# Hybrid block on one core: paired subtractions, gate parts on ScalarE and a deeper ring of raw weights in a linear-attention kernel

## The chip, the core and the metric

The program runs on 1 core of one Trainium2 chip. It uses TensorE (PE, matrix products; its weight loads are listed apart as PEld), VectorE (DVE), ScalarE (ACT), GpSimd (POOL) and the DMA queue of SyncE (SP). Each engine works through its own list of instructions in order and waits where one of them needs a result of another engine. The metric is the device time of the whole program in microseconds (us), as the median of several runs.

## The reference

Two transformer blocks follow each other on 512 tokens of width 1024. The first has two feed-forward layers and, between them, a mixer over 512 latent tokens and 256 context tokens. Half of that mixer is an HGRN2 linear attention with 4 heads of 128 channels, run in both directions. The second block has a Mamba2 mixer, a sparse attention and a mixture of experts. What the change touches computes this, for each head and direction:

```
q     = silu(hg_q) * 128 ** -0.5
log_f = log(lb + (1 - lb) * sigmoid(f_pre))
k_in  = (1 - lb) * sigmoid(-f_pre)
# per chunk, in token order:
b      = cumsum(log_f)
decay  = exp(b[t] - b[s])            for s <= t
scores = einsum('td,tsd,sd->ts', q, decay, k_in)
o      = scores @ v + (q * exp(b)) @ state
state  = exp(b_last) * state + (k_in * exp(b_last - b)).T @ v
```

The parts of the second block that matter here are `ada = silu(c) @ w_ada + b_ada` (a row of 6144 numbers out of a weight of 1024 x 6144) and its norm and projections `(rmsnorm(h) * (1 + scale) + shift) @ w_in`.

## The kernel before

Activations lie transposed, channels on the partitions and tokens along the row. Every large product is done as three products of split operands (`mm3`, L212 to L214): a weight is loaded as `wraw` (L183), rounded to `whi` on ACT (L193), and its rest `wlo` is formed on DVE (L194). The order of the instructions on each engine comes from a list scheduler that runs over the whole program with estimated durations and priorities (`later`, `high_priority`), so that an edit in one place can move instructions of other places.

**The HGRN2 stage** (`mix1`, 860 to 1120 us) goes through the 4 heads. `hg_front` (L881 to L943) makes for one head the projections, the gates and their prefix sums, in two directions `d`; `hg_back` (L945 to L1108) makes the attention. While `hg_back` of one head runs, `hg_front` of the next is in the lists too.

In `hg_front` the projection of the forget gate lands in two PSUM tiles, one of 512 latent and one of 256 context tokens. With p for it, DVE writes min(p, 0) and min(-p, 0) into slots 0 and 1 of `W` (L911, L912), ACT takes the exponential of both in one instruction of 1536 columns (L914), POOL adds them into slot 2 (L915), DVE writes slot 1 times lb plus slot 0 into slot 0 (L916), and ACT takes the logarithm of slots 0 and 2 (L917). DVE then reads p again (L921), which frees the PSUM tile, and forms log_f (L922), its prefix sum (`tensor_tensor_scan`, L927 or L932) and the second array (L929 or L934). Both land in one tile `BA` of four rows.

In `hg_back` the 512 x 512 decay is not formed. Seven levels m = 64, 32, ..., 1 split the sequence in blocks of 2m tokens; in each, queries of one half meet keys of the other, both measured from the border between them. For m < 64, two DVE subtractions fill the two halves of a tile `z` of 512 columns (L979, L980; the second reference is subtracted the other way round), ACT takes the exponential of the whole tile (L982), DVE multiplies the query half by q (L983), and PE does small products of `z` with itself (L988, L993, L999). DVE masks the small ones (L1003) and sums them (L1082), POOL copies the sums into the score tile (L1084), and PE finishes the head (L1089 to L1091), after which a norm follows (`hsq`, L1094; `rstdl`, L314; `rstd`, L319; `ho`, L1099). Six levels in two directions and four heads give 48 pairs of subtractions.

ACT keeps a table for the functions in use. A logarithm after an exponential, or the other way round, stands behind an ACT_TABLE_LOAD where the compiled list has one.

**The stage behind it** (1120 to 1200 us) finishes the mixer's output and computes the remaining rows of `ada`: `matvec` (L259 to L288) loads pieces of 512 KB into a ring of `mraw` tiles in the pool `xq` (L241), and PE multiplies them (L267). The ring has 6 tiles there (`MR = 6`). Two further parts of the row, `ada_row`, 8 pieces in all, run after the second feed-forward layer (L1809, L1816), at the start of the sparse attention near 1550 us, where the copy of their sums, `mvs`, is on ACT (L250). The memory of `xq` is used again by the tiles of the sparse attention, among them the weights `cw` (L1511).

Of the kernel before, what the change touches and what calls it, by code (L numbers as in the profile page):

```python
# [15 lines left out]
AF = mybir.ActivationFunctionType  # L16
OP = mybir.AluOpType
# [13 lines left out]
L = 512  # L31
C = 256
T = L + C
# [455 lines left out]
XA, XU, HPL = 0, 1, ()  # L489


class Mix1:
# [391 lines left out]
    def hg_front(self, i, w, vec, h):  # L884

        nc, hs = self.nc, self.hs
        PE = lambda k: nc.gpsimd if k in HPL else nc.vector
        lb = vec["lb"]
        q = hs.tile([128, L], F32, name="q", bufs=2)
        g = hs.tile([128, L], F32, name="g", bufs=2)  # L890

        def act(dst):
            def ev(p, t0, n):
                nc.scalar.activation(dst, p, AF.Tanh, scale=0.5)
                nc.vector.scalar_tensor_tensor(dst, dst, 1.0, p, op0=OP.add, op1=OP.mult)
            return ev
        self.proj_T(self.wsplit(self.cols(w, h * 128, 128), [8, 128], 2 in WL), self.LAT, act(q))

        BA = hs.tile([128, 4, T], F32, name="BA", bufs=2)
        Tt = hs.tile([128, 2, 12], F32, name="Tt", bufs=2)  # L900
        ks = hs.tile([128, L], F32, name="ks", bufs=2)
        for d in range(2):
            wt = self.wsplit(self.cols(w, 1536 + d * 512 + h * 128, 128), [8, 128], 3 + d in WL)
            col = slice(d * 4 + h, d * 4 + h + 1)
            W = hs.tile([128, 1 + 3 * T], F32, name="W", bufs=1)
            Wv = W[:, 1:].rearrange("p (s t) -> p s t", s=3)
            ps = []

            def evf(p, t0, n):
                ps.append((p, t0, n))  # L910
                nc.vector.tensor_scalar(Wv[:, 0, t0:t0 + n], p, 0.0, None, op0=OP.min)  # L911
                nc.vector.tensor_scalar(Wv[:, 1, t0:t0 + n], p, -1.0, 0.0, op0=OP.mult, op1=OP.min)  # L912
            self.proj_T(wt, self.ALL, evf)
            nc.scalar.activation(Wv[:, 0:2], Wv[:, 0:2], AF.Exp)  # L914
            nc.gpsimd.tensor_tensor(Wv[:, 2], Wv[:, 0], Wv[:, 1], op=OP.add)  # L915
            nc.vector.scalar_tensor_tensor(Wv[:, 0], Wv[:, 1], lb[:, col], Wv[:, 0], op0=OP.mult, op1=OP.add)  # L916
            nc.scalar.activation(Wv[:, 0:3:2], Wv[:, 0:3:2], AF.Ln, bias=self.tiny)  # L917
            lf, nk = Wv[:, 0], Wv[:, 1]
            for p, t0, n in ps:
                s = slice(t0, t0 + n)  # L920
                nc.vector.scalar_tensor_tensor(nk[:, s], p, 0.0, Wv[:, 2, s], op0=OP.max, op1=OP.add)  # L921
            PE(("l", d)).tensor_tensor(lf, lf, Wv[:, 2], op=OP.subtract)  # L922
            B, A = BA[:, 1 + d], BA[:, 3 * d]
            B64 = B.rearrange("p (b t) -> p b t", t=64)
            lno = vec["lno"][:, col]
            if d == 0:
                nc.vector.tensor_tensor_scan(B, self.rst64, lf, 0.0, op0=OP.mult, op1=OP.add)  # L927
                nc.vector.tensor_copy(Tt[:, d], B64[:, :, 63])
                nc.vector.scalar_tensor_tensor(A, nk, lno, B, op0=OP.subtract, op1=OP.add)  # L929
            else:  # L930
                nc.gpsimd.memset(W[:, 0:1], 0.0)
                nc.vector.tensor_tensor_scan(B, W[:, 0:T], self.rst64, 0.0, op0=OP.add, op1=OP.mult)  # L932
                nc.vector.tensor_add(Tt[:, d], B64[:, :, 63], lf.rearrange("p (b t) -> p b t", t=64)[:, :, 63])
                nc.vector.scalar_tensor_tensor(A, B, lno, nk, op0=OP.add, op1=OP.subtract)  # L934

            k = ks if d == 0 else Wv[:, 1, :L]
            nc.scalar.activation(k, nk[:, :L], AF.Exp, scale=-1.0, bias=lno)
            if d == 1:
                PE("k").tensor_tensor(ks, ks, k, op=OP.add)
        self.proj_T(self.wsplit(self.cols(w, 1024 + h * 128, 128), [8, 128], 5 in WL), self.LAT, act(g))  # L940
        for _ in range(FB[1]):
            self.filler()
        return q, g, BA, Tt, ks  # L943

    def hg_back(self, vec, h, mrg, front):  # L945
        nc, hs = self.nc, self.hs
        PE = lambda k: nc.gpsimd if k in HPL else nc.vector
        q, g, BA, Ta, ks = front
# [7 lines left out]
        for d in range(2):  # L956
            B, A, Tt = BA[:, 1 + d, :L], BA[:, 3 * d, :L], Ta[:, d, :8]
            X, Y = BA[:, 2 * d, :L], BA[:, 2 * d + 1, :L]
            sq, sk = (1, 0) if d == 0 else (0, 1)
            pds = [self.pt("pb") for _ in range(2)]  # L960
            nl = 6 - d
            for li, m in enumerate(LV + ([0] if d == 0 else [])):
                if m:
                    zz = hs.tile([128, L], F32, name="z", bufs=ZB)
                    half = lambda t: t.rearrange("p (b u t) -> p b u t", u=2, t=m)
                    zv, v, x, y = half(zz), half(B), half(X)[:, :, 0, :], half(Y)[:, :, 1, :]
                    nb = L // (2 * m)
                    if m == 64:
                        tv = Tt.rearrange("p (b u) -> p b u", u=2)
                        nc.vector.tensor_tensor(zv[:, :, 0, :], tv[:, :, 0:1].to_broadcast([128, nb, m]), x, op=OP.subtract)  # L970
                        if XA:
                            nc.scalar.activation(zv[:, :, 1, :], y, AF.Exp)
                            nc.scalar.activation(zv[:, :, 0, :], zv[:, :, 0, :], AF.Exp)
                        else:
                            nc.gpsimd.tensor_copy(zv[:, :, 1, :], y)
                    else:
                        r = v[:, :, 0, m - 1:m] if d == 0 else v[:, :, 1, 0:1]
                        r = r.to_broadcast([128, nb, m])
                        PE(("x", d, m)).tensor_tensor(zv[:, :, 0, :], r, x, op=OP.subtract)  # L979
                        PE(("y", d, m)).tensor_tensor(zv[:, :, 1, :], y, r, op=OP.subtract)  # L980
                    if m != 64 or not XA:
                        nc.scalar.activation(zz, zz, AF.Exp)  # L982
                    PE(("q", d, m)).tensor_tensor(zv[:, :, sq, :], zv[:, :, sq, :], half(q)[:, :, sq, :], op=OP.mult)  # L983
                for c in range(4):
                    t0 = c * 128
# [9 lines left out]
                    else:  # L995
                        x = ((c % 2) * nl + li - 2) * 32
                        for b in range(4):
                            s = slice(t0 + b * 32, t0 + b * 32 + 32)
# [40 lines left out]
            else:  # L1039
                nc.vector.memset(off[:, 0], 0.0)  # L1040
                for b in (1, 2, 3):
# [3 lines left out]
                                    op=OP.subtract if d == 0 else OP.add)  # L1045
# [13 lines left out]
            p = self.pt("pb")  # L1059
# [7 lines left out]
            for a, b in zip(order[:-1], order[1:]):  # L1067
                n = cs.index(a)
                nc.vector.scalar_tensor_tensor(st[:, b, :], st[:, a, :], eT[:, a:a + 1], p[:, n * 128:(n + 1) * 128],
                                               op0=OP.mult, op1=OP.add)  # L1070
# [9 lines left out]
        for half in range(2):  # L1080
            r = hs.tile([128, 2, 32], F32, name="dr", bufs=2)
# [1259 lines left out]
MA = (0, 1)  # L2341
# [22 lines left out]
class Top:  # L2364
# [41 lines left out]
    def first(self, i, b1, lat, mrg, xd, x1d, cosd, sind, row):  # L2406
# [107 lines left out]
        with tc.tile_pool(name="xq", bufs=1, reuse_waits="tile") as xq:  # L2514
# [1 line left out]
            for o in range(KC):  # L2516
                nc.sync.dma_start(xT[:, o, :], xd[:, o, :])
            out_half(0, lambda o: xT[:, o, :], lambda o, x: None, OA)
            self.mvp, self.ptag, self.mva = xq, "pb", MA[0]
            for f in self.fill + [row.pop(0) for _ in range(FN)]:  # L2520
                f()
            a, b = scales(6, "n3", 1)
# [65 lines left out]
```

## Time and profile before

| | |
|---|---|
| median of 3 runs | 2819.61 us (2817.72 to 2821.18) |
| profiled execution, its own time | 2824.22 us |
| span of its profile | 2822.4 us |
| busy over the span: PE / DVE / ACT / POOL | 94% / 55% / 35% / 10% |
| granted TensorE clock, mean | 0.975 of full speed |
| DMA | 380.46 MB, mean 135 GB/s |

The page divides busy time by the whole span, and stages with different limits are mixed in it: DVE has 55% over all, and much more in some stretches. So the stretches are read one by one, by the busy time of each engine between two times, and then by what each engine waited for there. In the timelines a row shows the start, the duration, the engine, the line, the operation and the tiles; behind it in brackets stands the idle time before it and the instruction that ended it. An instruction's duration overlaps with the start of the next, so that the distance between two starts is what one costs its engine.

### The profile page before, as it was taken

To read this page: it belongs to the slowest core of one execution; us is meant where nothing else is said; L and a number is where in the kernel's file an instruction comes from. 1 tells how busy PE (TensorE), PEld (TensorE's weight loads), DVE (VectorE), ACT (ScalarE), POOL (GpSimd) and SP (SyncE) were. 2 spreads that over 40 slices of the span, in tenths; PEclk is the share of its full clock that TensorE was granted. 3 is DMA by queue.
4 is the path that set the end of the run, shared out by engine and by line. 5 is a ranking of instruction groups with operands and counts; after the bars stand their busy time and mean duration, and the time that the engine had idled before them with its cause. 6 is when DMAs were issued, how large, how long until landed. Compare 5 with 4: busy or idle time off the path is not lost. (4 is left out here: it accounts for less than half of the span.)

```text
span 2822.4 us, 40841 instructions
## 1 busy us (share of the span) xinstructions
PE 2666.9 (94%) x16161; PEld 2055.5 (73%) x16162; DVE 1549.1 (55%) x3025; ACT 995.6 (35%) x1796; POOL 279.3 (10%) x319
## 2 busy tenths in 40 slices
PE   7999999999998887999999899999999989979998
PEld 5788888888887765678888678777777767854443
DVE  6333333338367885554434757676667764454444
ACT  5211112225235663422222424465444443231112
POOL 2000000002001210100000101121122230010000
PEclk9999999999999988999999999999999999989999
DMA  7422122134333228732333523301234358269995
GB/s 263 150 90 68 58 63 67 46 98 119 98 104 100 65 81 268 254 97 90 98 96 87 153 83 98 92 13 36 76 104 123 97 185 256 82 228 368 368 359 213
DMA packets 341571, 380.46 MB, mean 135 GB/s; under 512 B 21881, under 2 KB 252669, under 8 KB 341122
## 3 DMA queue, kind: packets, MB, share of 16 engines
q1 hardware_dynamic: 339074, 373.63, 41.1%
q0 software_dynamic: 2304, 4.20, 0.5%
q8 instruction: 128, 2.10, 0.3%
q14 instruction: 65, 0.53, 0.1%
HBM read 352.34 MB, written 29.63 MB: 135 GB/s over the span
## 5 line engine op out<-in xcount | busy, mean ns | idle before, releaser
L193 ACT CAST whi<-wraw 128x1024 fp32r<-128x1024 f32 x277 | 285.8, 1042 | 742.4 <-PE pppa L213 332.5
L212 PE MATMUL pppa<-lath,whi 128*128 128x512 f32 (+4 forms) x1344 | 522.4, 390 | 18.2 <-ACT lath L1835 5.0
L213 PE MATMUL pppa<-latl,whi 128*128 128x512 f32 (+3 forms) x1344 | 520.0, 387 | 6.4 <-DVE latl L360 4.3
L214 PE MATMUL pppa<-lath,wlo 128*128 128x512 f32 (+3 forms) x1344 | 513.3, 384 | 0.0
L194 DVE TENSOR_TENSOR wlo<-wraw,whi 128x1024 fp32r<-128x1024 f32 (+1 forms) x273 | 332.9, 1225 | 244.4 <-ACT whi L193 239.8
L212 PEld LDWEIGHTS pppa<-lath,whi 128*128 128x128 f32 (+3 forms) x1344 | 256.1, 191 | 81.4 <-ACT whi L193 10.8
L213 PEld LDWEIGHTS pppa<-latl,whi 128*128 128x128 f32 (+2 forms) x1344 | 255.6, 190 | 63.4 <-DVE latl L360 7.6
L214 PEld LDWEIGHTS pppa<-lath,wlo 128*128 128x128 f32 (+2 forms) x1344 | 255.2, 190 | 50.9 <-issue 2.8
L213 PE MATMUL pppb<-hl,whi 128*128 128x512 f32 (+1 forms) x576 | 195.6, 341 | 0.0
L212 PE MATMUL pppb<-hh,whi 128*128 128x512 f32 (+1 forms) x576 | 193.2, 345 | 0.0
L214 PE MATMUL pppb<-hh,wlo 128*128 128x512 f32 (+1 forms) x576 | 190.9, 340 | 0.0
L418 DVE SCALAR_TENSOR_TENSOR xT<-pppb,sG,xT 128x512 f32<-128x512 f32 (+1 forms) x144 | 96.7, 689 | 137.4 <-PE pppb L214 137.3
L398 DVE TENSOR_TENSOR hf<-sg,pppa 128x256 f32<-128x256 f32 (+1 forms) x68 | 39.6, 583 | 228.6 <-PE pppa L214 227.3
L212 PE MATMUL pppf<-lath,whi 128*128 128x512 f32 x320 | 128.0, 400 | 6.9 <-ACT lath L1835 3.1
L212 PE MATMUL pppa<-ctxh,whi 128*128 128x256 f32 (+1 forms) x440 | 124.0, 282 | 7.0 <-DVE W L921 7.0
L212 PEld LDWEIGHTS pppb<-hh,whi 128*128 128x128 f32 x576 | 108.2, 189 | 28.1 <-issue 5.8
L2143 PE MATMUL pppa<-ew,xg 128*64 128x512 f32 x512 | 128.4, 607 | 0.0
L214 PE MATMUL pppf<-lath,wlo 128*128 128x512 f32 x320 | 126.7, 396 | 0.6 <-DVE wlo L194 0.6
L213 PE MATMUL pppf<-latl,whi 128*128 128x512 f32 x320 | 126.8, 396 | 0.1
L213 PE MATMUL pppa<-ctxl,whi 128*128 128x256 f32 (+1 forms) x440 | 123.6, 281 | 0.4 <-POOL ctxl L358 0.4
L214 PE MATMUL pppa<-ctxh,wlo 128*128 128x256 f32 (+1 forms) x440 | 123.5, 281 | 0.0
L213 PEld LDWEIGHTS pppb<-hl,whi 128*128 128x128 f32 x576 | 108.9, 189 | 15.6 <-issue 3.4
(694 smaller groups left out, 4985.4 us busy)
## 6 DMA issues: line engine op xcount, KB each, us to landing
wraw<-in_ffn_w_dram SPq DMA_DIRECT2D x132, 512.0 KB, 4.0
wraw<-in_w_in_dram SPq DMA_DIRECT2D x102, 512.0 KB, 4.0
ew<-in_w_exp_gate_dram SPq DMA_DIRECT2D x64, 512.0 KB, 8.6
ew<-in_w_exp_up_dram SPq DMA_DIRECT2D x64, 512.0 KB, 4.8
ew<-in_w_exp_down_dram SPq DMA_DIRECT2D x32, 1024.0 KB, 11.0
mraw<-in_w_mod_dram SPq DMA_DIRECT2D x40, 512.0 KB, 6.2
wraw<-in_w_mod_dram SPq DMA_DIRECT2D x32, 512.0 KB, 4.2
mraw<-in_w_ada_dram SPq DMA_DIRECT2D x32, 512.0 KB, 5.6
```

Source lines behind the costliest of these rows:

```text
L193: nc.scalar.copy(hi[:, :n], raw[:, :n])
L194: (nc.gpsimd if pool else nc.vector).tensor_sub(lo[:, :n], raw[:, :n], hi[:, :n].bitcast(F32))
L212: nc.tensor.matmul(out, wh, xh, start=start, stop=False)
L213: nc.tensor.matmul(out, wh, xl, start=False, stop=False)
L214: nc.tensor.matmul(out, wl, xh, start=False, stop=stop)
L398: nc.vector.tensor_mul(h[:, :n], sg[:, :n], pp[1])
L418: nc.vector.scalar_tensor_tensor(x[:, o, :], p[:, :n], gate[:, o:o + 1], x[:, o, :], op0=OP.mult, op1=OP.add)
L2143: nc.tensor.matmul(ph[x * 64:x * 64 + 64, :], xg[:, k, x * 64:x * 64 + 64], wts[k // 4 * 2 + x][:, :, k % 4, :], start=(k == 0), stop=(k = ...
```

## The change

It has three parts. In `hg_front`, ACT writes max(-p, 0) and max(p, 0) by Relu straight from PSUM instead of DVE's two minima, the exponential takes them with scale -1, and the two combinations behind it change places: DVE writes the weighted sum into slot 2 and POOL then the plain sum into slot 0. In `hg_back`, one DVE subtraction of 512 columns fills both halves of `z` for m < 64; its first operand is a view that runs from the first row of `BA` to the next at every half block. The sign goes into the exponential, which is taken in two instructions, one for each half. For the third part the ring of `mraw` tiles has 8 instead of 6 from 1120 us on.

```diff
@@ hg_front
             def evf(p, t0, n):
                 ps.append((p, t0, n))
-                nc.vector.tensor_scalar(Wv[:, 0, t0:t0 + n], p, 0.0, None, op0=OP.min)
-                nc.vector.tensor_scalar(Wv[:, 1, t0:t0 + n], p, -1.0, 0.0, op0=OP.mult, op1=OP.min)
+                nc.scalar.activation(Wv[:, 0, t0:t0 + n], p, AF.Relu, scale=-1.0)
+                nc.scalar.activation(Wv[:, 1, t0:t0 + n], p, AF.Relu)
             self.proj_T(wt, self.ALL, evf)
-            nc.scalar.activation(Wv[:, 0:2], Wv[:, 0:2], AF.Exp)
-            nc.gpsimd.tensor_tensor(Wv[:, 2], Wv[:, 0], Wv[:, 1], op=OP.add)
-            nc.vector.scalar_tensor_tensor(Wv[:, 0], Wv[:, 1], lb[:, col], Wv[:, 0], op0=OP.mult, op1=OP.add)
+            nc.scalar.activation(Wv[:, 0:2], Wv[:, 0:2], AF.Exp, scale=-1.0)
+            nc.vector.scalar_tensor_tensor(Wv[:, 2], Wv[:, 1], lb[:, col], Wv[:, 0], op0=OP.mult, op1=OP.add)
+            nc.gpsimd.tensor_tensor(Wv[:, 0], Wv[:, 0], Wv[:, 1], op=OP.add)
             nc.scalar.activation(Wv[:, 0:3:2], Wv[:, 0:3:2], AF.Ln, bias=self.tiny)
...
-                nc.vector.scalar_tensor_tensor(nk[:, s], p, 0.0, Wv[:, 2, s], op0=OP.max, op1=OP.add)
-            PE(("l", d)).tensor_tensor(lf, lf, Wv[:, 2], op=OP.subtract)
+                nc.vector.scalar_tensor_tensor(nk[:, s], p, 0.0, Wv[:, 0, s], op0=OP.max, op1=OP.add)
+            PE(("l", d)).tensor_tensor(lf, Wv[:, 2], lf, op=OP.subtract)
@@ hg_back
                         r = v[:, :, 0, m - 1:m] if d == 0 else v[:, :, 1, 0:1]
-                        r = r.to_broadcast([128, nb, m])
-                        PE(("x", d, m)).tensor_tensor(zv[:, :, 0, :], r, x, op=OP.subtract)
-                        PE(("y", d, m)).tensor_tensor(zv[:, :, 1, :], y, r, op=OP.subtract)
-                    if m != 64 or not XA:
+                        r = r[:, :, None, :].to_broadcast([128, nb, 2, m])
+                        a = BA[:, 2 * d, :L]
+                        xy = bass.AP(tensor=a.tensor, offset=a.offset, ap=[a.ap[0], [2 * m, nb], [T + m, 2], [1, m]])
+                        nc.vector.tensor_tensor(zv, xy, r, op=OP.subtract)
+                        nc.scalar.activation(zv[:, :, sq, :], zv[:, :, sq, :], AF.Exp, scale=2.0 * sq - 1.0)
+                        nc.scalar.activation(zv[:, :, sk, :], zv[:, :, sk, :], AF.Exp, scale=2.0 * sk - 1.0)
+                    if m == 64 and not XA:
                         nc.scalar.activation(zz, zz, AF.Exp)
@@ Top.first
-            self.mvp, self.ptag, self.mva = xq, "pb", MA[0]
+            self.mvp, self.ptag, self.mva, self.mvn = xq, "pb", MA[0], 8
```

In the changed file L916 is DVE's weighted sum and L917 POOL's sum; L912 and L913 are the two Relus, L915 the exponential, L918 the logarithm, L922 the second read of p, L983 the joint subtraction, L984 and L985 the exponentials of the halves, L987 that of level 64, L988 the product with q. Below L985 the lines are five further down than before.

On DVE, where the first direction's gates of the second head meet the end of the first head's attention, the list before reads:

```order
L911 TENSOR_SCALAR W<-pppa 128x256
L912 TENSOR_SCALAR W<-pppa 128x256
L983 TENSOR_TENSOR z<-z,q 128x256
L916 SCALAR_TENSOR_TENSOR W<-W,lb 128x768
L1003 TENSOR_TENSOR dg<-pppb,dmask 128x2x160 x2
L1082 TENSOR_REDUCE dr<-dg 128x64 x2
L921 SCALAR_TENSOR_TENSOR W<-pppa,W 128x512
L921 SCALAR_TENSOR_TENSOR W<-pppa,W 128x256
```

and now (L1008 is the old L1003, L1087 the old L1082, L1074 the old L1069, an update of the running state):

```order
L983 TENSOR_TENSOR z<-BA 128x512
L988 TENSOR_TENSOR z<-z,q 128x256
L1008 TENSOR_TENSOR dg<-pppb,dmask 128x2x160 x2
L1087 TENSOR_REDUCE dr<-dg 128x64 x2
L916 SCALAR_TENSOR_TENSOR W<-W,lb 128x768
L1074 SCALAR_TENSOR_TENSOR st<-st,eT,pppb 128x128 x3
L922 SCALAR_TENSOR_TENSOR W<-pppa,W 128x512
L922 SCALAR_TENSOR_TENSOR W<-pppa,W 128x256
```

The masks and sums now stand ahead of the weighted sum, and the state updates stand between it and the second read of p.

On ACT, the list before in the following direction-0 levels of the second head (`fq` and `fk` are the exponentials for the running state):

```order
L914 ACTIVATE W<-W 128x1536
L982 ACTIVATE z<-z 128x512 x6
L1019 ACTIVATE fq<-BA 128x4x64
L1026 ACTIVATE fk<-fk 128x512
L1094 ACTIVATE hsq<-pppb 128x512
L894 ACTIVATE g<-pppa 128x512
L917 ACT_TABLE_LOAD
L917 ACTIVATE W<-W,tiny 128x2x768
L314 ACTIVATE rstdl<-pppb,eps 128x512
L1020 ACT_TABLE_LOAD
```

and now:

```order
L912 ACTIVATE W<-pppa 128x256
L913 ACTIVATE W<-pppa 128x256
L987 ACTIVATE z<-z 128x512
L984 ACTIVATE z<-z 128x8x32
L985 ACTIVATE z<-z 128x8x32
L314 ACT_TABLE_LOAD
L314 ACTIVATE rstdl<-pppb,eps 128x512
L984 ACT_TABLE_LOAD
L984 ACTIVATE z<-z 128x16x16
L915 ACTIVATE W<-W 128x1536
L985 ACTIVATE z<-z 128x16x16
```

The logarithm of the earlier head's norm has moved between two levels and has two table loads of its own. In the whole list there are 62 table loads instead of 56; the six more all lie in this stage.

On SP, at the start of the sparse attention (`w2t` are small weights of it, `g2d` is the finished piece of the row), the list before:

```order
L1529 DMA w2t<-in_cmp_w_k_dram 128x2x64
L1529 DMA w2t<-in_cmp_w_v_dram 128x2x64
L241 DMA mraw<-in_w_ada_dram 128x2x512 x2
L1529 DMA w2t<-in_cmp_w_v_dram 128x2x64
L1818 DMA g2d<-ada 1x512
L1814 DMA ada<-in_b_ada_dram 1x512
L1818 DMA g2d<-ada 1x512
```

and now:

```order
L183 DMA wraw<-in_w_in_dram 128x8x48
L183 DMA wraw<-in_w_in_dram 128x8x128 x6
L1823 DMA g2d<-ada 1x512
L1819 DMA ada<-in_b_ada_dram 1x512
L1823 DMA g2d<-ada 1x512
L1233 DMA cmneg<-in_k_cmneg_dram 128x128
```

The last two pieces of `mraw` are gone from this place; they are issued with the others near 1190 us. The first loads of `cw` and the `w2t`, which stood here and just above, come later, behind the constants of the sparse attention.

## Rows read from the trace of the kernel before

**Rows 1.** Busy time per engine: one head, then the stage; granted clock; DMA.

```profile
core 0: us, PE busy (x) PEld busy (x) DVE busy (x) ACT busy (x) POOL busy (x), PEclk, DMA share, GB/s
917.60:972.30 54.70, 48.68 (x622) 39.53 (x621) 48.38 (x104) 34.79 (x57) 10.75 (x15) 0.91 0.30 83
...
860.00:1070.00 210.00, 177.88 (x2239) 142.56 (x2239) 182.84 (x392) 135.21 (x216) 41.14 (x47) 0.90 0.32 94
```

**Rows 2.** What PE waited for, 860 to 1070 us: total us, times, longest.

```profile
PE pppf L988 <- DVE z L983: 8.8, 5, 3.4
PE pppa L212 <- DVE W L921: 7.0, 4, 2.2
```

**Rows 3.** DVE timeline: the weighted sum and the wait before it.

```profile
919.48 1.02 DVE L916 SCALAR_TENSOR_TENSOR W<-W,lb 128x768 f32<-128x768 f32 x1 [3.22 <-POOL W L915]
```

**Rows 4.** What DVE waited for, 860 to 1120 us.

```profile
DVE W L916 <- POOL W L915: 13.8, 4, 3.6
```

**Rows 5.** DVE timeline: minima, subtractions, a product of 512, a state update.

```profile
912.65 0.67 DVE L1029 TENSOR_TENSOR fq<-fq,q 128x512 f32<-128x512 f32 x1
913.25 1.00 DVE L1003 TENSOR_TENSOR dg<-pppb,dmask 128x384 f32<-128x384 f32 x2
...
928.86 0.33 DVE L1069 SCALAR_TENSOR_TENSOR st<-st,eT,pppb 128x128 f32<-128x128 f32 x1
...
929.87 0.68 DVE L912 TENSOR_SCALAR W<-pppa 128x512 f32<-128x512 f32 x1
930.47 0.41 DVE L911 TENSOR_SCALAR W<-pppa 128x256 f32<-128x256 f32 x1
...
933.14 2.07 DVE L980 TENSOR_TENSOR z<-BA 128x256 f32<-128x256 f32 x1
935.13 0.41 DVE L979 TENSOR_TENSOR z<-BA 128x256 f32<-128x256 f32 x1
935.47 0.41 DVE L980 TENSOR_TENSOR z<-BA 128x256 f32<-128x256 f32 x1
```

**Rows 6.** ACT timeline: logarithms, a table load, exponentials of 256 and 512, a copy from PSUM.

```profile
940.32 1.58 ACT L917 ACTIVATE W<-W,tiny 128x1536 f32<-128x1536 f32 x1
941.81 0.67 ACT L314 ACTIVATE rstdl<-pppb,eps 128x512 f32<-128x512 f32 x1
942.50 1.28 ACT L1020 ACT_TABLE_LOAD   x1
943.79 0.42 ACT L1020 ACTIVATE fq<-fq 128x256 f32<-128x256 f32 x1
944.11 0.61 ACT L982 ACTIVATE z<-z 128x512 f32<-128x512 f32 x1
944.63 0.61 ACT L319 ACTIVATE rstd<-rstdl 128x512 f32<-128x512 f32 x1
...
945.51 0.58 ACT L247 COPY mvr<-pppa 128x512 f32<-128x512 f32 x1
```

**Rows 7.** Line L980: durations in ns (min/median/max), first and last start in us.

```profile
L980 DVE TENSOR_TENSOR z<-BA x48: 407/411/2381, 877.8 to 1076.1; 128x256 f32<-128x256 f32 x48
```

**Rows 8.** POOL timeline: its sum, first and second direction.

```profile
917.59 1.85 POOL L915 TENSOR_TENSOR W<-W 128x768 f32<-128x768 f32 x1 [10.69 <-ACT W L914]
...
932.87 2.06 POOL L915 TENSOR_TENSOR W<-W 128x768 f32<-128x768 f32 x1 [3.70 <-ACT W L914]
```

**Rows 9.** What PE waited for, 1530 to 1660 us.

```profile
PE pppb L1809 <- DMA mraw<-in_w_ada_dram: 5.3, 1, 5.3
```

**Rows 10.** DVE timeline: the start of the second half's norm.

```profile
1567.51 0.42 DVE L2544 TENSOR_TENSOR r<-rf 128x256 f32<-128x256 f32 x1 [2.61 <-ACT rf L319]
```

**Rows 11.** ACT timeline: the copy of the row's sums.

```profile
1566.58 0.59 ACT L250 COPY mvs<-pppb 128x512 f32<-128x512 f32 x1 [2.18 <-PE pppb L1809]
```

**Rows 12.** Line L1516: durations in ns (min/median/max), first and last start in us.

```profile
L1516 PE MATMUL pppb<-cw,ks x64: 379/379/482, 1645.5 to 1662.5; 128*63 128x256 f32 x64
```

**Rows 13.** What SP's queue waited for, 1060 to 1260 us.

```profile
SPq L241 <- PE pppb L267: 30.3, 15, 6.3
```

## The prediction

> **What bounds the kernel now.** Over the whole span PE is busy 94% of the time, so only a stretch in which PE stands idle can give anything. I read busy time by stretch first. From 860 to 1070 us, the HGRN2 stage, PE is busy 177.88 of 210 us [rows 1], so 32 us are idle, and the granted clock is 0.90. DVE is busy 182.84 of the same 210, and within one head (917.6 to 972.3, from one sum of POOL's for direction 0 to the next) 48.38 of 54.7. ACT has 34.79 there. The list of PE's waits comes next: 8.8 us are for the first product of `z` with q and 7.0 for DVE's second read of the gate's PSUM tile [rows 2], together 15.8 of the 32, both behind DVE's own list. So DVE sets the pace of a head here, and PE follows it. Last I read DVE's waits: 13.8 us, four times 3.45, are for POOL's sum ahead of the weighted sum in direction 0 [rows 3, 4]. Nothing else on DVE is idle for long, so what leaves DVE's list shortens the head until another engine is later.
>
> **Gate parts to ACT.** A minimum of 512 columns costs DVE 0.60 us (929.87 to 930.47) and for one of 256 columns I take the 0.34 of a subtraction of that size (935.13 to 935.47), with the same duration of 0.41 [rows 5]. A head has four of each, 2.40 + 1.36 = 3.8 us. ACT takes as many Relus from PSUM. The nearest row is a copy of 512 columns from PSUM, 0.58 [rows 6]; for 256 I take the 0.42 of an exponential. That makes 4.0 us a head on an engine with 20 us free, and the exponential behind them no longer waits for another engine. The list shows no table load ahead of a Relu, so none is counted.
>
> The Trainium skill, "ScalarE: Activation LUTs", section "Rules for kernel authors", says to do relu, max and min on VectorE and not on ScalarE. The rows do not bear it out for this fp32 operand in PSUM: 0.68 for DVE's minimum, 0.58 for ACT's copy. By the rule the move would be a loss wherever ACT is late; the first rival below has that case from rows.
>
> **One subtraction for two.** The pair costs 2 x 0.34, and a product of 512 columns with both operands in SBUF costs 0.60 (912.65 to 913.25) [rows 5]. The saving is 0.08, twelve times a head, 0.9 us. No row of this kernel shows an operand that runs back and forth between two rows of a tile, and that stands as a rival. On ACT one exponential of 512 (0.52 from 944.11 to 944.63) becomes two of 256 (0.32 from 943.79 to 944.11) [rows 6]: 0.12 more, 1.4 us a head.
>
> **The sum's place.** DVE's weighted sum no longer waits for POOL. The logarithm now does, and the second read of p waits for that. Between the two on DVE lie POOL's 1.85 [rows 8] and the logarithm's 1.58 [rows 6], 3.4 us, in which DVE has only three state updates of 0.33 [rows 5]. The masks and sums that used to stand there now fill the time of the exponential instead. So a wait of 3.45 becomes one of about 2.4, a gain of 1.0 a head. Behind this wait on DVE stand the whole prefix sum and all subtractions of direction 0, and PE's next context projection waits for the PSUM tile, as it did. In direction 1 POOL's sum still runs beside DVE: a subtraction of 0.41 takes 2.07 while POOL runs its 2.06 [rows 5, 8]. I count no change there.
>
> **The table loads.** Six more loads at 1.28 [rows 6] are 7.7 us of ACT. They come in pairs around the logarithm of the previous head's norm, now between the exponentials of levels 32 and 16. From the joint subtractions on, DVE has some 4.9 us of its own (five subtractions 3.0, two parts of `fk` 0.7, the product `fq` 0.6, two products 0.7) before it wants level 16. ACT has in that time level 64 (0.52), two halves (0.64), load, logarithm, load (3.24), one half (0.32), the gate's exponential (about the 1.58 of a logarithm of equal size) and the other half (0.32), 6.6 us. So DVE waits some 1.7 us a head. If the pair hid altogether this would be 0; if the norm's sum came late as well, it would be the pair's whole 3.24.
>
> The same page of the Trainium skill, section "What ACT_TABLE_LOAD costs", gives 1283 ns for the load and 1380 ns more for a drain. Here the load has the first figure, and of the second nothing is seen: the logarithm before ends at 942.48, the load starts at 942.50, and the exponential behind starts 0.01 after its end [rows 6]. With the drains a pair of loads would hold up ACT by 2.8 us more a head; if DVE waited for all of it, three heads' worth would be 8 us, and the forecast near 2813, on the side of the first rival below.
>
> **Sum for the stage.** Per head 3.8 + 0.9 + 1.0 - 1.7 = 4.0 us. Two full heads give 8.0. In the first head part of PE's wait is the gate's chain itself, which keeps its length, so I count half, 2.0. In the last there is no next head: one direction of minima (1.9), the pairs (0.9) and the wait (1.0) less 1.7 make 2.1. That is 12.1, inside the 15.8 that PE waits for DVE.
>
> **Eight raw tiles.** At 1563 us PE waits 5.3 us for a piece of `mraw` [rows 9]. The last two pieces of the row had no free tile earlier; with eight they have. Next late is the norm of the second half. Its DVE chain starts after a wait of 2.61 [rows 10], because on ACT the copy `mvs` stands ahead and waits 2.18 for those very products [rows 11]. So the chain of the norm moves up by about 2.6, and the projections end with it. I take 2.6, between 0 (the norm is as late as before) and 5.3. The moved `cw` loads are first used at 1645.5 [rows 12], some 50 us after their new place; I count nothing. At 1120 us the ring's waits lie on SP (30.3 us in 15 waits [rows 13], 2 us a piece) and none of PE's long waits is for a piece. Two pieces more stand ahead of the next layer's weights, which costs at most 4 if those were just in time, and gains at most 2; I take 0, since PE works on other products there.
>
> Together 14.7 us. On the profiled execution's own 2824.2 that gives 2809.5; the median of the runs is 4.6 lower (2819.6), and the same difference gives 2805.
>
> **Rivals.** First, ACT takes DVE's place. It gets 4.0 + 1.4 + 1.9 = 7.3 us a head more, 42 of 54.7 busy. For it: it works in order, and `z` goes DVE, ACT, DVE. Against it: half of it lies where DVE is busy with other things. If all 7.3 stood in DVE's way instead of 1.7, a head would lose 1.6 rather than gain 4.0; over three heads' worth that is +5, less 2.6: 2822. If two thirds do (4.9), a head gains 0.8 and the total is near 2815. I give this case 0.18, around 2818.
>
> Second, the joint subtraction is slow. If an operand that changes rows every m columns cost 1.2 us instead of 0.6, 48 of them would add 29 us to the list that bounds: 2805 + 29 = 2834. It decides from 0.9 us each on, where the 14.7 are gone; slower than before above that. Against it: the old subtractions run from level 32, in runs of 32 columns, down to level 1, which reads every second column, and all but those beside POOL's work cost the same, 407 ns at the least and 411 in the median [rows 7]. Chance 0.07.
>
> Third, DVE is relieved further than I count. The waits for table loads hide, PE's idle time shrinks by 24 of the 32 (the rest are chains that stay), and the 5.3 go whole: 2790. For it: the score sums and state updates now end earlier, so that PE can finish a head while it used to wait. Against it: ACT between the levels. Chance 0.15.
>
> **How the numbers follow.** My own case has 0.60, with 2798 to 2811. The range of 8 in 10 reaches to the third rival and over most of the first, 2790 to 2817. What a measurement of this kernel can tell from no change is about 0.2%, 5.6 us. Faster by more than that: 0.60 + 0.15 and a quarter of the first rival, 0.80. Within it: the rest of the first rival, 0.13. Slower: 0.07.
>
> **What would show it.** From one direction-0 sum of POOL's to the next should be near 51 us instead of 54.7; no minima on DVE; L983 near 0.67 in duration; DVE's wait for POOL replaced by one of 2 to 3 us for the logarithm; DVE waiting for ACT at level 16; the wait for `mraw` near 1560 gone. I am wrong if L983 takes 0.9 or more, if DVE's waits for ACT exceed 5 us a head, or if PE's idle time from 860 to 1070 stays above 28 us.

## The result, and the profile after

The changed kernel takes 2839.49 us (median of 4 runs, 2837.51 to 2841.86), the kernel before 2818.66 beside it: a ratio of 1.0073, 95% interval 1.0057 to 1.0088, so 20.6 us slower. The forecast was 14.7 us faster, and its range ended at 2817. The profiled execution took 2837.51, with a span of 2835.7.

The busy time by stretch of the changed kernel comes first; it answers to [rows 1]. The first two rows are the second and third head, from one direction-0 sum of POOL's to the next:

```profile
921.35:979.00 57.65, 49.40 (x630) 39.18 (x628) 46.43 (x84) 41.11 (x78) 10.64 (x14) 0.91 0.28 79
979.00:1046.30 67.30, 58.75 (x604) 42.25 (x604) 45.30 (x83) 42.48 (x79) 9.22 (x15) 0.87 0.24 68
...
860.00:1070.00 210.00, 181.79 (x2148) 140.17 (x2147) 156.27 (x287) 142.66 (x267) 38.01 (x46) 0.93 0.26 73
```

A head lasts 57.65 and 67.30 us where it lasted 54.70, and 51 was forecast. DVE has fewer instructions in a head (84 for 104), its busy time in the second head fell by 2.0 us (48.38 to 46.43), and it is now idle 11 us of the 57.65, where it was idle 6.3. So a relief came, smaller than forecast, and the head became longer all the same. In the third head PE is *busy* 58.75 us with fewer products (604, where 622 took 48.68 in [rows 1]). The granted clock, 0.87 for 0.91, accounts for some 2 us of that, an estimate from the two busy times. A PE that is busier with less work points to its list and not to a wait.

The same view from the table load at L854 to that at L396, which is the HGRN2 stage and most of the one behind it, before and then changed:

```profile
849.15:1175.14 325.99, 281.48 (x2927) 215.96 (x2926) 247.10 (x515) 180.04 (x292) 55.41 (x67) 0.90 0.47 146
850.87:1191.27 340.40, 292.24 (x2922) 219.27 (x2921) 235.41 (x435) 203.52 (x377) 54.29 (x67) 0.91 0.46 143
```

This stretch is 14.4 us longer at nearly the same granted clock. PE is busy for 10.8 of them, with as many products, and idle for 3.6. DVE is busy 11.7 us less and ACT 23.5 us more.

PE's timeline of the third head, with gaps between the rows shown:

```profile
1016.15 0.39 PE L213 MATMUL pppa<-latl,whi 128*128 128x512 f32 x1
1016.38 0.39 PE L214 MATMUL pppa<-lath,wlo 128*128 128x512 f32 x1
...
1024.41 0.50 PE L212 MATMUL pppa<-lath,whi 128*128 128x512 f32 x1
1024.84 0.25 PE L1004 MATMUL pppb<-z 128*32 128x32 f32 x2
1025.02 0.49 PE L213 MATMUL pppa<-latl,whi 128*128 128x512 f32 x1
...
1034.12 0.39 PE L213 MATMUL pppa<-ctxl,whi 128*128 128x256 f32 x1
1034.44 0.25 PE L1004 MATMUL pppb<-z 128*32 128x32 f32 x2
1034.62 0.38 PE L214 MATMUL pppa<-ctxh,wlo 128*128 128x256 f32 x1
```

Two large products of 512 columns start 0.23 us apart. With one small product of a level between them it is 0.61 (1024.41 to 1025.02); for 256 columns it is 0.50 (1034.12 to 1034.62), where two neighbours in the kernel before are 0.115 apart. Each insertion costs 0.38 us. In a group the small product is nearly free: 32 records, which are 16 products with two records each, take 0.46. The weight loads (PEld) show how:

```profile
1015.92 0.19 PEld L213 LDWEIGHTS pppa<-latl,whi 128*128 128x128 f32 x1
...
1025.02 0.19 PEld L213 LDWEIGHTS pppa<-latl,whi 128*128 128x128 f32 x1
1025.44 0.14 PEld L1004 LDWEIGHTS pppb<-z 128*32 128x32 f32 x2 [0.24 <-issue]
```

Without insertions the load for the product at 1016.15 runs 0.23 us ahead, beside the product before. With them it starts with its own product, at 1025.02, and before the small product's load, at 1025.44, the loading of weights stands idle for 0.24 us. So nothing is loaded ahead, in either direction. The Trainium skill, "TensorEngine Tiling (Array Packing)", section "Key Properties", says that a change of tiling mode drains TensorE; these rows agree with it, at 0.38 us for going to 32 columns and back, though no row shows the drain as such.

From 1022.31 to 1040.48 there are 30 such places, whose starts add up to 11.6 us above the plain distance. The kernel before has none here. In PE's list (L1004 is the small product) this stood as follows, and it could have been read before the run:

```
L212 MATMUL pppa<-lath,whi 128x512
L1004 MATMUL pppb<-z 32x32
L213 MATMUL pppa<-latl,whi 128x512
L1004 MATMUL pppb<-z 32x32
L214 MATMUL pppa<-lath,wlo 128x512
```

The masks behind the spread products start late. The row of DVE's timeline for the first one:

```profile
1036.70 0.49 DVE L1008 TENSOR_TENSOR dg<-pppb,dmask 128x320 f32<-128x320 f32 x1 [11.90 <-PE pppb L1004]
```

DVE's list of waits, 860 to 1070 us, answers to [rows 4]:

```profile
DVE dg L1008 <- PE pppb L1004: 16.5, 4, 11.9
DVE W L922 <- ACT W L918: 15.8, 8, 3.6
DVE W L916 <- ACT W L915: 8.6, 4, 3.9
DVE z L988 <- ACT z L984: 5.4, 4, 2.8
```

The list of the kernel before has, beside the 13.8 us for POOL, two of these waits for ACT:

```profile
DVE z L983 <- ACT z L982: 4.1, 2, 2.0
DVE W L921 <- ACT W L917: 3.6, 2, 2.0
```

The 13.8 us for POOL are gone. The waits for ACT at these places are 29.8 us (15.8 + 8.6 + 5.4) where they were 7.7. ACT's timeline of the second head shows what is in the way, and answers to [rows 6]:

```profile
930.65 0.60 ACT L912 ACTIVATE W<-pppa 128x512 f32<-128x512 f32 x1 [0.98 <-DVE T L1014]
931.14 0.60 ACT L913 ACTIVATE W<-pppa 128x512 f32<-128x512 f32 x1
...
932.55 0.66 ACT L987 ACTIVATE z<-z 128x512 f32<-128x512 f32 x1
933.07 0.44 ACT L984 ACTIVATE z<-z 128x256 f32<-128x256 f32 x1
933.38 0.43 ACT L985 ACTIVATE z<-z 128x256 f32<-128x256 f32 x1
933.83 1.28 ACT L314 ACT_TABLE_LOAD   x1
935.12 0.69 ACT L314 ACTIVATE rstdl<-pppb,eps 128x512 f32<-128x512 f32 x1
935.83 1.28 ACT L984 ACT_TABLE_LOAD   x1
937.13 0.42 ACT L984 ACTIVATE z<-z 128x256 f32<-128x256 f32 x1
937.45 1.47 ACT L915 ACTIVATE W<-W 128x1536 f32<-128x1536 f32 x1
```

DVE in the same time (answers to [rows 5]), and the line of the joint subtraction (ns, to [rows 7]):

```profile
931.30 3.09 DVE L983 TENSOR_TENSOR z<-BA 128x512 f32<-128x512 f32 x5
...
937.58 0.42 DVE L988 TENSOR_TENSOR z<-z,q 128x256 f32<-128x256 f32 x1 [1.18 <-ACT z L984]
...
938.95 1.02 DVE L916 SCALAR_TENSOR_TENSOR W<-W,lb 128x768 f32<-128x768 f32 x1 [0.88 <-ACT W L915]
```

```profile
L983 DVE TENSOR_TENSOR z<-BA x48: 675/680/1765, 878.0 to 1094.6; 128x512 f32<-128x512 f32 x48
```

The five subtractions are done by 934.4, and then the levels stand behind ACT's pair of table loads: DVE waits 1.18 us for the exponential of level 16 and 0.88 for that of the gate. A subtraction of 512 columns over the two rows takes 0.68, as forecast. PE's list of waits from 1530 to 1660 us no longer has the raw piece, against [rows 9]:

```profile
PE pppa L213 <- POOL latl L358: 2.5, 1, 2.5
PE pppa L213 <- DVE latl L360: 1.2, 3, 0.6
```

### The profile page after: what moved, and what is told of

It reads as the page before. It is cut to its first block, busy times and chain, and to the rows that moved or that the text cites. A ratio compares the mean times of both kernels' runs of the same rounds, so it can differ in the third digit from the quotient of the medians.

```text
span 2835.7 us, 40871 instructions
## 1 busy us (share of the span) xinstructions
PE 2686.0 (95%) x16161; PEld 2064.0 (73%) x16162; DVE 1533.5 (54%) x2945; ACT 1018.3 (36%) x1882; POOL 282.8 (10%) x319
## 5 line engine op out<-in xcount | busy, mean ns | idle before, releaser
L212 PE MATMUL pppa<-lath,whi 128*128 128x512 f32 (+3 forms) x1344 | 522.5, 390 | 18.3 <-ACT whi L193 8.9
L212 PEld LDWEIGHTS pppa<-lath,whi 128*128 128x128 f32 (+2 forms) x1344 | 255.0, 190 | 83.6 <-ACT whi L193 16.7
```

What stands on the lines that cost most here:

```text
L212: nc.tensor.matmul(out, wh, xh, start=start, stop=False)
```

## The experiments

"Lone" is the number of small products (levels 16 to 1 and the diagonal) that stand alone between two large ones in PE's list, "loads" that of table loads in the HGRN2 stage of ACT's list. The ratio is that to runs of the kernel before beside it. The difference is the ratio less one, times 2819, and two rows are compared by it.

| kernel | lone | loads | median us | ratio (95%) | difference |
|---|---|---|---|---|---|
| before | 0 | 16 | 2818 to 2820 | | |
| changed | 28 | 22 | 2839.5 | 1.0073 (1.0057-1.0088) | +20.6 |
| e1 changed, grouped | 0 | 22 | 2817.2 | 1.0003 (0.9991-1.0015) | +0.8 |
| e2 gate part alone | 33 | 22 | 2840.0 | 1.0086 (1.0070-1.0103) | +24.2 |
| e3 joint subtraction alone | 0 | 22 | 2821.8 | 1.0015 (1.0005-1.0025) | +4.2 |
| e4 eight raw tiles alone | 0 | 16 | 2818.3 | 1.0001 (0.9990-1.0012) | +0.3 |
| e5 changed, 440 places | 3 | 22 | 2826.5 | 1.0021 (1.0010-1.0031) | +5.9 |
| e6 before, 380 places | 30 | 18 | 2831.2 | 1.0034 (1.0022-1.0046) | +9.6 |
| e7 e1 without the joint subtraction | 0 | 22 | 2809.3 | 0.9964 (0.9950-0.9978) | -10.1 |
| e8 e1 with DVE's minima | 0 | 16 | 2800.7 | 0.9926 (0.9910-0.9943) | -20.9 |
| e9 before, eight tiles, grouped | 0 | 16 | 2805.9 | 0.9957 (0.9945-0.9969) | -12.1 |
| e10 e8 without the joint subtraction | 0 | 22 | 2823.9 | 1.0017 (1.0006-1.0028) | +4.8 |
| e11 e8 and Relus of q | 0 | 20 | 2820.4 | 1.0012 (1.0000-1.0023) | +3.4 |
| e12 changed, DVE's minima | 24 | 20 | 2838.0 | 1.0075 (1.0056-1.0094) | +21.1 |
| e13 e8 and 12 table loads | 0 | 28 | 2824.7 | 1.0018 (1.0007-1.0030) | +5.1 |
| e14 e1, one table at the norm | 0 | 20 | 2806.7 | 0.9946 (0.9934-0.9958) | -15.2 |
| e15 e8, 440 places | 0 | 16 | 2811.8 | 0.9964 (0.9951-0.9977) | -10.1 |

**e1, the small products grouped.**

```diff
+                            with self.tc.high_priority(offset=200):
                                 nc.tensor.matmul(pds[c // 2][b * 32:b * 32 + 32, x:x + 32], ...
```

> The changed kernel, with the small products of levels 16 to 1 and of the diagonal issued at a higher priority, so that they stand together again and not one by one between the projections of the next head. Theory A (the loss is PE's order: 30 lone small products in the fourth head's projections, each 0.38 us because the next large product starts at 0.61 instead of 0.23 and at 0.49 instead of 0.11): 11 us back, about 2828. Theory B (ACT has taken DVE's place, Relus and table loads hold up the levels): no change, 2836 to 2842. Theory C (the granted clock): the gain is below 4 us and the stretch 1015 to 1045 still shows PE busy without gaps.

It gave 20 us back, more than theory A's 11. The surplus has its own control in e9. In its trace the third head, from one direction-0 sum of POOL's to the next, lasts 58.7 us (980.42 to 1039.13), 8.6 less than in the change. PE's timeline at the corresponding place:

```profile
1031.35 0.28 PE L212 MATMUL pppa<-ctxh,whi 128*128 128x256 f32 x1
1031.55 0.49 PE L1003 MATMUL pppb<-z 128*32 128x32 f32 x32
```

A group of 32 records now takes about what a single insertion cost (0.38).

**e2, e3, e4: one part at a time.** Each is the kernel before with one part of the change's own diff.

> The kernel before with the gate part alone (Relus on ACT, the two sums change places). In the list 33 lone small products now stand between large ones. Theory A: their 12.5 us and a gain of at most 8 from DVE's relief make 2823 to 2832. Theory B: the four Relus a head add 4 us of ACT, 16 in four heads, of which the head sees some: 2819 to 2835 as well, but then PE's idle time from 860 to 1070 is larger than 32 us.

> The kernel before with the joint subtraction alone. No lone small products in the list, 62 table loads. Theory A: the joint subtraction saves DVE little (0.08 for each) and costs ACT 0.12 for each, six table loads more: within 4 us of before, 2815 to 2823. Theory B: the two exponentials and the table loads lie in the way of the levels: 5 to 10 us slower, 2824 to 2829.

> The kernel before with eight raw tiles alone: the wait for the raw piece near 1560 us goes, and 2 to 3 us with it: 2816. If the moved loads of the sparse attention's weights cost something: 2818 to 2822.

The gate part alone is as slow as the whole change, slower than either theory said, and brings the lone products (35 places and 14.7 us above the plain distance in its trace). Theory B's sign is missing: PE is idle 31.2 us from 860 to 1070, not more than 32. The joint subtraction alone loses 4, inside theory A's range. The eight tiles change nothing that can be measured; the 2.6 forecast is at the edge of the interval.

**e5 and e6: the same list effect from the other side.**

```diff
-HGL = 420
+HGL = 440   (e5, on the changed kernel; e6: HGL = 380 on the kernel before)
```

> The changed kernel with the next head's front end set back by 440 instead of 420 places in the scheduler's priorities. In PE's list 3 lone small products are left instead of 28. Theory A (lone products): most of the 22 us that the block of e1_block gave back come back here too, 2817 to 2824. Rival (the block gained for another reason, the higher priority itself): 2834 to 2842.

> The kernel before, no part of the change in it, with 380 instead of 420 places. Its list has 30 lone small products between projections, which the kernel before has not, and 58 table loads instead of 56. Theory A: slower by 30 x 0.38 = 11 us at least and by 22 at most, 2829 to 2840. Rival: the lone products cost what they cost in a group, 2815 to 2821.

e5 takes 25 of the 28 lone products out and is 14.7 us faster than the change; its 2826.5 lies a little above theory A's range and far under the rival's. e6 is the cleanest one: nothing of the change is in it, though its list has two table loads more. Its trace has 30 lone places with 11.1 us above the plain distance, and it is 9.6 us slower than before. Rows of e6, PE's timeline:

```profile
975.52 0.38 PE L212 MATMUL pppa<-ctxh,whi 128*128 128x256 f32 x1
975.83 0.25 PE L999 MATMUL pppb<-z 128*32 128x32 f32 x2
976.01 0.39 PE L213 MATMUL pppa<-ctxl,whi 128*128 128x256 f32 x1
```

**e7 and e8: what holds the head once the products are grouped.**

```diff
 e8: on e1
-                nc.scalar.activation(Wv[:, 0, t0:t0 + n], p, AF.Relu, scale=-1.0)
-                nc.scalar.activation(Wv[:, 1, t0:t0 + n], p, AF.Relu)
+                nc.vector.tensor_scalar(Wv[:, 0, t0:t0 + n], p, 0.0, None, op0=OP.min)
+                nc.vector.tensor_scalar(Wv[:, 1, t0:t0 + n], p, -1.0, 0.0, op0=OP.mult, op1=OP.min)
```

> The kernel e1_block without the joint subtraction: gate part, eight raw tiles, small products in groups. If ACT now sets the pace of a head (theory D), the 48 pairs of exponentials that become single ones give ACT 5.8 us back: 2812 to 2815. If not (theory E, the head is as long as the chain from the gate over the levels to PE), 2815 to 2820.

> The kernel e1_block with DVE's minima instead of the Relus (the two sums still change places, the joint subtraction and eight raw tiles stay, small products in groups). The list has 56 table loads instead of 62. Theory D (ACT sets the pace): ACT gets 4.0 and 1.9 us a head less, 2805 to 2811. Theory E: 2815 to 2820. If DVE is still the bound, the minima cost 3.8 us a head, 2822 to 2832.

Both are faster than either theory said: e8 is 21.7 us faster than e1, more than theory D gave, and is the fastest of all, the kernel before included. DVE's minima are not what bounds. The Relus are not priced by this alone, since e8's list also has six table loads fewer.

**e9, the control.** The priority of e1 and the eight tiles on the kernel before.

> The kernel before with eight raw tiles and the small products at the higher priority; PE's list of small products is in groups as before. A control for e1, e7 and e8: if the priority itself gains nothing, 2815 to 2821; if it gains (earlier score products), under 2813, and then part of what e7 and e8 gained is not the change's.

It gains 12.1 us by itself, so e1, e7, e8 and e14 are to be held against e9 and not against the kernel before. Held so, the change with its small products in groups (e1) is 12.9 us slower. The gain lies at the stage's end. PE's timeline of the kernel before there, and of e9:

```profile
1095.05 0.90 PE L999 MATMUL pppb<-z 128*32 128x32 f32 x76
...
1100.65 0.35 PE L999 MATMUL pppb<-z 128*32 128x32 f32 x4
```

```profile
1075.08 1.48 PE L1000 MATMUL pppb<-z 128*32 128x32 f32 x128
1076.74 0.50 PE L1000 MATMUL pppb<-z 128*32 128x32 f32 x32 [0.17 <-DVE z L983]
```

The last head's small products end some 24 us earlier. Behind them ACT squares the head's result for the last norm; its row before, and in e9:

```profile
1116.72 0.60 ACT L1094 ACTIVATE hsq<-pppb 128x512 f32<-128x512 f32 x1 [7.27 <-PE pppb L1091]
```

```profile
1101.01 0.60 ACT L1095 ACTIVATE hsq<-pppb 128x512 f32<-128x512 f32 x1 [1.79 <-PE pppb L1092]
```

It starts 15.7 us earlier.

**e10, e11, e12.** e10 takes the joint subtraction out of e8. e11 adds to e8 two Relus of q per gate tile, into a slot that is overwritten. e12 is the changed kernel with DVE's minima and no grouping.

```diff
 e11: on e8
                 ps.append((p, t0, n))
+                for _ in range(2):
+                    nc.scalar.activation(Wv[:, 2, t0:t0 + n], q[:, :n], AF.Relu)
```

> e8 without the joint subtraction: DVE's minima, the two sums change places, eight raw tiles, small products in groups; 62 table loads. If the two sums' places are what gained in e8: 2799 to 2808. If the joint subtraction gained it (48 fewer DVE instructions, 0.1 us each, and shorter chains): 2811 to 2818.

> e8 with as many Relus on ACT as the change has, of the same sizes, but of q, into a slot of W that is overwritten later (extra work, the output is not changed): their operand is there long before, so ACT spends their time, 4.0 us a head, but does not wait for PE's projection with the levels' exponentials behind it. If ACT's time is the bound: 2812 to 2818, as in e1. If its waiting in order is (theory F, the Relu at the head of ACT's list waits for the projection's end): 2800 to 2806. Its list has 60 table loads.

> The changed kernel with DVE's minima instead of the Relus, nothing set for the small products: 24 lone ones stand in its list, 60 table loads. Theory A prices 24 x 0.38 = 9 us on the 2800.7 of e8: 2808 to 2818. If the Relus alone made the change slow, near 2801.

e11 speaks against theory F: Relus that wait for nothing cost as much, though four table loads came with them. e10, e11 and e12 all came out slower than every expectation. In all three the loads had gone up from 16 to 20 or 22, and that made the next two experiments.

**e13 and e14: the table loads.**

```diff
 e13: on e8, at the head of the loop over the levels
+                if m == 16 and d == 0 and h:
+                    self.table("natural_log")
+                    self.table("exp_and_others")
 e14: on e1
-        rs = self.rstd(pn_, L, 128)
+        rs = self.rstd(pn_, L, 128, both=True)
```

> e8 with one pair of table loads more ahead of level 16 of direction 0 in heads 1 to 3 (where the changed kernel's list has its pair), which gives 28 loads in the stage instead of 16 since three later ones change places too. No Relu on ACT. If table loads are what e1 pays for: 12 x 1.28 = 15 us of ACT, of which half or more shows, 2808 to 2817. If they hide beside DVE and PE: 2799 to 2804.

> e1 with one table for logarithm and exponential loaded ahead of each head's norm: 20 loads in the stage instead of 22, and none left between the levels 32 and 16 where the norm's logarithm is. If the loads between the levels are what e1 pays for: 2806 to 2812. If the Relus' time on ACT is: 2814 to 2819.

With twelve loads more e8 is 26 us slower, which is more than the 15 us that they take on ACT. This is no price of a load, though the average is 2.2. From one direction-0 sum of POOL's to the next, e13's second head is no longer than e8's, 57.2 us and 58.0, although the pair stands in it; its third is 11.1 longer. In its last head 12 products of levels 64 and 32, which the table does not count, stand singly between large ones, 4.6 us above the plain distance, and e8 has none of these. And e3, with six loads more, is 4.2 us slower in all. One table for both functions at the norm gave e1 16 us back, with all Relus still on ACT; in the single traces the stretch from L854 to L396 is 8.7 us shorter (311.1 for 319.8). The trace has seven loads fewer, four of them behind the HGRN2 stage. ACT's timelines of e13 and of e14 at that place:

```profile
934.66 0.41 ACT L986 ACTIVATE z<-z 128x256 f32<-128x256 f32 x1
935.08 2.57 ACT L310 ACT_TABLE_LOAD   x2
937.66 0.42 ACT L985 ACTIVATE z<-z 128x256 f32<-128x256 f32 x1
```

```profile
934.35 0.65 ACT L985 ACTIVATE z<-z 128x512 f32<-128x512 f32 x1
934.88 0.71 ACT L314 ACTIVATE rstdl<-pppb,eps 128x512 f32<-128x512 f32 x1
935.44 0.45 ACT L982 ACTIVATE z<-z 128x256 f32<-128x256 f32 x1
```

In e14 the norm's logarithm stands in the middle of the exponentials without a load on either side. That agrees with what the Trainium skill, "ScalarE: Activation LUTs", section "Rules for kernel authors", says on kernels that need both functions: take the table that holds exponential and logarithm together.

**e15, e8 at 440 places.**

> e8 with 440 instead of 420 places between the heads' priorities: small products in groups, 56 loads. If e8's gain is that of its parts and not of one lucky list: 2797 to 2805. If it is luck: 2806 to 2820.

Both counts are as in e8, and yet 10.8 of e8's 20.9 us are gone, though not the sign. PE's timeline shows a part of it that the count leaves out: nine products of levels 64 and 32 stand singly in the last head, 3.6 us above the plain distance, which e8 has not. Three rows of it:

```profile
1082.55 0.51 PE L214 MATMUL pppa<-lath,wlo 128*128 128x512 f32 x1
1082.98 0.33 PE L991 MATMUL pppf<-z 128*64 128x64 f32 x2
1083.24 0.51 PE L212 MATMUL pppa<-lath,whi 128*128 128x512 f32 x1
```

So the order of the list is worth some 10 us by ways that the two counts do not catch, and differences of that size between two experiments are not to be put down to their edit.

## Why the prediction was wrong

**What bounds.** That DVE was the fullest engine behind PE's waits was read rightly for the list before, though "nothing else on DVE is idle for long" passed over the 7.7 us that it waited for ACT. What failed is the half sentence "what leaves DVE's list shortens the head until another engine is later": two others were later at once. That DVE's work sets the pace is not shown by any run, since e8 puts the minima back on DVE and is the fastest. DVE's relief was smaller, too. In the second head 4.7 us of its work were to go (3.8 + 0.9), and 2.0 went. The minima are off it, and the subtractions take 2.3 us less. But six subtractions of one column, `off` (L1043 and L1047), take 4.27 us instead of 0.42: two of them now stand beside POOL's work and last 1.78 (940.22) and 2.37 (963.12). Before, a subtraction of `z` stood there [rows 5, 8].

**A term that was missing: PE's own list.** The sum counted what leaves DVE and what comes to ACT, and took PE's list as it was. The scheduler places the whole program anew, and the next head's projections met the small products at equal priority. That is 11.6 us in the trace, and 10.8 of the 14.4 us from L854 to L396 are busy time of PE. e6 shows it without the change at 9.6, and e5 takes most of it away. e1 and e9 together fit it, if the priority is worth the same in both (19.8 back, 12.1 of them the priority's own, 7.7 left for the lone products). No rival had it.

**The term that was mis-sized: the sum's place.** A gain of 1.0 us a head was forecast. POOL's wait of 3.45 was to become one of 2.4 for the logarithm, and the wait for the exponential was put at nothing, because masks and sums would fill its time. Over the stage 13.8 us for POOL and 3.6 for the logarithm became 8.6 for the exponential and 15.8 for the logarithm: 7.0 more, where 4 less were forecast. For PE this and the table loads show as 3.6 us more of idle time from L854 to L396.

**The table loads** were sized about right at the place where the prediction looked: behind the pair DVE waits 2.1 us in the second head (1.18 + 0.88), where 1.7 was taken. What the Relus, the loads and the order cost further down ACT's list was not taken apart. Together they are the 12.9 us of e1 against e9, of which by the estimate below some 6 go with the granted clock. With one table at the norm (e14) or with the minima back and six loads fewer (e8) these come back, 16.0 and 21.7. The Trainium skill, "ScalarE: Activation LUTs", section "What ACT_TABLE_LOAD costs", has 1380 ns of drain besides the 1283 of a load. In e13 two loads in a row take 2.57 us and the exponential follows 0.01 later, so no drain is seen.

**The prediction's own signs.** Two of the three signs of being wrong came: DVE's waits for ACT are 7.5 us a head (29.8 over four) where 5 was the limit, and PE's idle time from 860 to 1070 is 28.2 where 28 was. The joint subtraction stayed at 0.68.

**The first rival** (ACT takes DVE's place, 0.18, about 2818) had the right mechanism for the second loss: the waits for ACT went from 7.7 to 29.8 us. I held it too small, because I counted ACT's busy time (42 of 54.7 forecast, 41.11 of 57.65 measured) and not what stands in order behind a load.

**Gate parts to ACT.** The Relu of 512 costs 0.49 (930.65 to 931.14 in ACT's timeline) and the minima are off DVE, as forecast. No gain shows: e8, with the minima back on DVE, is 21.7 us faster than e1, and 5.7 faster than e14, which is less than the order of a list can be worth. The Trainium skill, "ScalarE: Activation LUTs", section "Rules for kernel authors", says to do relu on VectorE and not on ScalarE. e8 agrees with the rule, though not by the price of one instruction (0.49 on ACT, 0.60 on DVE [rows 5]).

**One subtraction for two.** The duration holds, and the second rival (slow across rows) is out at 0.68 us. The gain of this part and of the sum's place is not shown. e8 against e9, which differ in these two, is 8.8 us faster, where about 6 were forecast; but at 440 places (e15) it is 2.0 slower than e9, and the joint subtraction alone (e3) is 4.2 slower than the kernel before.

**Eight raw tiles.** The wait went, but the 2.6 us are not seen in e4 (-2.8 to +3.4).

**The granted clock** stands in theory C of e1, but no experiment holds it fixed. In the two traces it is about the same from L854 to L396 (0.90 and 0.91), so the 14.4 us there are not its doing. The runs differ in it. Its mean over the span is 0.969 to 0.972 in those of the change, 0.976 on the average in those of the kernel before and 0.980 in those of e8. Among the runs of one kernel, 0.001 less goes with 1.6 us more (one line fitted through all of them). By that, an estimate, some 8 of the change's 20.6 us go with the clock, 4 of e9's 12, and of the distances from e8 some 7 of e13's 26, 9 of e11's 24 and 4 of e15's 10.8. Why the lists differ in it stays open.

**Left open:** e12 is 42 us above e8, of which 24 lone products (9), the priority (12) and four loads at e13's average (9) are 30; by the estimate above some 12 go with the clock (0.972 for 0.980), and these terms overlap. e7 gains 10.9 against e1 where e10 loses 25.7 against e8, by the same edit; six loads at e13's average would be 13 of the latter. What else the order of the list does, as in e15, was not taken apart.

## What to carry to other kernels

When a scheduler places the program, compare the list of every engine, the fullest one first, and look for instructions of another shape that now stand singly between large products, and for table loads that now stand inside a loop. A knob such as the 420 places here can sit just beside an edge: the kernel before is 9.6 us slower at 380. Where a part of a change is to be judged, hold both sides at the same list properties, and look at the granted clock of the runs, or it is the list that is measured.

## What the runs showed of the hardware

A small product of 32 columns between two large ones costs 0.38 us, whether the large ones have 512 or 256 columns, and in a group of 32 records 0.46 us for all. PE counts as busy in that time, so the busy share hides it. A product of 64 columns between two of 512 costs 0.46 (1082.55 to 1083.24 in e15, 0.69 for 0.23). Two table loads in a row take 2.57 us on ACT, and the exponential behind them starts 0.01 later (e13). A DVE subtraction of one column takes 0.15 us, and 1.78 where it stands beside POOL's sum (940.22 in the change).
